# Low parts of expert weights: the last 256 columns of each 1536-column chunk subtracted on GpSimd, the rest on VectorE

## The chip, the core and the metric

The kernel runs on one core of one Trainium2 chip. The metric is the device time of one execution in microseconds (us). In the profile TensorE is PE (its weight loads PEld), VectorE is DVE, ScalarE is ACT, GpSimd is POOL, and SyncE, which issues the large loads, is SP. SBUF is the on-chip memory from which all of them read, PSUM the one into which PE writes.

## The reference

Two layers of a decoder run on 256 positions of width 1024 in float32: attention and a short convolution with a dense feed-forward block, then a gated spatial layer with a feed-forward block of 8 experts, of which each token uses the best two. The part that matters here is the experts:

```python
def expert_block(args):
    xb, e = args
    return (jax.nn.silu(xb @ w1[e]) * (xb @ w3[e])) @ w2[e]
```

For each expert w1 and w3 are 1024x2816 and w2 is 2816x1024. All eight experts together have 277 MB of float32 weights, and every weight is read once.

## The kernel before

To keep float32 accuracy in matmuls of the rounded type `float32r`, each operand is split in two: a high part (the rounded copy) and a low part (the value less its high part). A product is high by high, high by low and low by high.

**The weight stream.** The class `Stream` (L49) brings all weights in, in the order in which PE uses them. SP loads raw tiles of up to 3072 columns (1.5 MB, L126) into a ring, which for the experts has 7 tiles (`RAWA` and `RAWB`). `convert` (L138) takes a raw tile in chunks of 1536 columns (`CVC`): ACT writes the high part `whi` (L153), and DVE subtracts it from the raw weights to give the low part `wlo` (L154). `whi` and `wlo` have four buffers each (`CVA`). `take` (L161) hands 512 or 384 columns at a time to PE. Before it begins a new chunk it calls `convert`, so that conversion is up to four chunks ahead, counting the one that PE is about to use. The chunk that comes four later needs the buffers that PE frees. When the last chunk of a raw tile is converted, `prefetch` (L110) issues the next load into the ring, and that load waits until the tile has been read.

**The experts** (`experts`, L1237) go through 8 experts in three column steps each (1024, 1024 and 768 of the 2816 columns). In each step `up` (L1119) multiplies by w1 and w3, and `down` (L1185) multiplies the step before by w2. Experts 0, 2, 4 and 6 hold up to 128 tokens and take three matmuls for each 512 columns of weights (L447 to L449). Experts 1, 3, 5 and 7 hold up to 64, whose high and low parts lie side by side in one operand, so two matmuls suffice (L1129 and L1130, L1196 and L1197), and the halves are added by `folded` (L1150). A chunk of 1536 columns is thus nine matmuls of 512 columns or six. Besides `wlo`, DVE has small work there on PSUM results: L1145, L1172, L1182, L1210 and L1220. L1168 alone reads two SBUF tiles, as L154 does.

**The order** of DVE, ACT and POOL is fixed by hand from L927 to L1274: each of the three executes in the order of the program text. POOL issues three small loads near the end of the experts (`tail_loads` and `tail_gf`, L1285 to L1290, through L492 and L220) and has nothing else in that stage. After the experts six chunks of 1536 columns for the last projection go through the same stream. Before L913 chunks are converted in two halves of 768 columns (`st.parts` is 2); from there on whole.

Of the kernel before, what the change touches and what calls it, by code (L numbers as in the profile page):

```python
# [10 lines left out]
F32 = mybir.dt.float32  # L11
# [21 lines left out]
CVC = 1536  # L33
RAWA, RAWB = 4, 3
CVA, CVB = 4, 1
# [13 lines left out]
class Stream:  # L49
# [3 lines left out]
    def __init__(self, nc, raws, cvs, cols=RAWC, fixed=None):  # L53
        self.nc, self.raws, self.cvs, self.cols, self.fixed = nc, raws, cvs, cols, fixed
        self.specs, self.loaded, self.n_load = [], [], 0
        self.chunks, self.ready, self.n_conv = [], [], 0
        self.cur, self.pos, self.n_use = None, 0, 0
        self.spare = {}
        self.base, self.ahead, self.parts, self.stop = 0, len(cvs), 1, None

    def add(self, parts, lens):
        i = len(self.specs)
        self.specs.append(parts)
        off = 0
        for n in lens:
            self.chunks.append((i, off, n))
            off += n
# [70 lines left out]
    def convert(self):  # L138
        while self.n_conv < min(self.stop or len(self.chunks), self.n_use + self.ahead):
            ti, off, n = self.chunks[self.n_conv]  # L140
            idx, raw = self.loaded[0]
            assert idx == ti
            base, raw = [u for u in raw if u[0] <= off][-1]
            if self.fixed:
                hi, lo = self.fixed[1]
            else:
                cp = self.cvs[self.n_conv % len(self.cvs)]
                hi = cp.tile([P, CVC], F32R, tag="whi", name="whi")
                lo = cp.tile([P, CVC], F32R, tag="wlo", name="wlo")
            m = self.parts if n % (256 * self.parts) == 0 else 1  # L150
            for i in range(m):
                a, b = n * i // m, n * (i + 1) // m
                self.nc.scalar.activation(hi[:, a:b], raw[:, off - base + a:off - base + b], AF.Copy)  # L153
                self.nc.vector.tensor_sub(lo[:, a:b], raw[:, off - base + a:off - base + b], hi[:, a:b].bitcast(F32))  # L154
            self.ready.append((hi, lo, n))
            self.n_conv += 1
            if self.n_conv == len(self.chunks) or self.chunks[self.n_conv][0] != ti:
                self.loaded.pop(0)
                self.prefetch()
# [14 lines left out]
def decoder_trunk(ctx: ExitStack, tc: tile.TileContext, x, p, positions, ln_mix, ln_ffn, ln_ple, a_w_in,  # L174
# [30 lines left out]
    def bank(name="bank", g="B"):  # L205
        return psp.tile([P, 512], F32, tag="bank" + g, name=name)
# [21 lines left out]
    st = Stream(nc, [(rawp, RAWA)], [cvp] * CVA + [cvp2] * CVB)  # L228
# [572 lines left out]
    for s in range(NSL):  # L801
# [10 lines left out]
        for i in range(len(ab)):  # L812
            n = min(2, nb - 2 * i)
# [24 lines left out]
    for q in range(2):  # L838
        b = bank("wsT")
# [47 lines left out]
    for i in range(4):  # L887
        b = bank("sgp")
# [10 lines left out]
        hi = sg.h[i // 2][:, (i % 2) * 2:(i % 2) * 2 + 2]  # L899
# [15 lines left out]
    st.prefetch()  # L915
    st.stop, st.ahead = None, CVA - 1
    st.convert()
    st.ahead = CVA


    hnh = [t4(dt=F32R, name="hnh") for _ in range(2)]
# [69 lines left out]
    b = bank("rk")  # L991
# [319 lines left out]
    with tc.If(most > 0):  # L1311
# [15 lines left out]
        st = Stream(nc, [], [None], 512, (raws, cvf))  # L1327
# [34 lines left out]
```

## Time and profile before

| what | value |
| --- | --- |
| median of 3 runs | 1207.97 us (1207.48 to 1208.82) |
| profiled execution | 1207.52 us, of which the span of the trace is 1205.3 us |
| busy PE, DVE, ACT, POOL | 1157.8, 974.7, 838.7, 38.5 us |
| data read from HBM | 358.26 MB, 298 GB/s over the span |

The profile is one execution, and its times are from the span's start. A busy PE is not PE at its peak, since ends of matmuls are modelled. A row of a timeline has the start, the duration, the engine, the line and operation, output and inputs with their shapes, how many in a row (x13), and in brackets the engine's idle time before it with what ended it. Instructions of one engine are pipelined: one that is ready begins a little before the end of the one before it, so the spacing of a run of them is shorter than their duration.

### The profile page before, as it was taken

How to read it: one execution, taken by the hardware profiler on the slowest of the kernel's cores; microseconds unless marked ns; L12 is line 12 of the kernel's file. 1: busy time of each engine (PE TensorE's matmuls, PEld its weight loads, DVE VectorE, ACT ScalarE, POOL GpSimd, SP SyncE). 2: the span in 40 equal slices, each digit the busy share in tenths (PEclk: the TensorE clock that was granted, in tenths of full speed). 3: DMA queues.
4: the chain of work that ended last, by engine and by line, in shares of the span. 5: the costliest groups of instructions: out<-in, count | busy, mean ns of one | idle time of the engine just before them, and what ended most of it. 6: DMA issues, size and time to landing. Idle time of an engine off the chain costs nothing.

```text
span 1205.3 us, 16666 instructions
## 1 busy us (share of the span) xinstructions
PE 1157.8 (96%) x6307; PEld 1002.0 (83%) x6307; DVE 974.7 (81%) x1027; ACT 838.7 (70%) x1010; POOL 38.5 (3%) x80
## 2 busy tenths in 40 slices
PE   7999999999999999999999999999999999999985
PEld 5888899998779888888888977888977888987864
DVE  6567756474576778889999989999989999989993
ACT  6645644353466457789887788888788888788864
POOL 1001000000010010000000000000000000000003
PEclk9999999999999979999999999999999999999998
DMA  9634555286546569899999989999989999999921
GB/s 325 222 113 162 195 169 175 89 298 245 163 148 211 209 240 385 334 344 395 403 409 405 407 307 408 399 409 406 397 317 406 377 411 405 398 339 391 395 113 38
DMA packets 112521, 360.46 MB, mean 299 GB/s; under 512 B 6577, under 2 KB 23089, under 8 KB 112434
## 3 DMA queue, kind: packets, MB, share of 16 engines
q1 hardware_dynamic: 110834, 353.56, 77.6%
q0 software_dynamic: 1600, 5.77, 1.5%
q8 instruction: 51, 0.84, 0.3%
q14 instruction: 36, 0.29, 0.1%
HBM read 358.26 MB, written 1.05 MB: 298 GB/s over the span
## 4 chain that ended last, share of the span: by engine, by line
PE 86%; DVE 7%; ACT 2%; issue 2%; POOL 1%; DMA 1%; SPq 0%; POOLq 0%; DVEq 0%; ACTq 0%
DVE wlo L154 4%; PE a L447 3%; PE a L448 3%; PE y L447 3%; PE a L449 3%; PE b L448 3%; PE b L449 3%; PE b L447 3%; PE y L448 3%; PE y L449 3%; PE b L1130 3%; PE gTp L1160 3%; PE y L1197 3%; PE y L1196 3%; PE b L1129 3%; PE a L1130 2%
## 5 line engine op out<-in xcount | busy, mean ns | idle before, releaser
L154 DVE TENSOR_TENSOR wlo<-raw,whi 128x1536 fp32r<-128x1536 f32 (+2 forms) x551 | 770.3, 1444 | 151.3 <-ACT whi L153 148.8
L153 ACT ACTIVATE whi<-raw 128x1536 fp32r<-128x1536 f32 (+2 forms) x551 | 660.8, 1238 | 247.9 <-issue 37.9
L1130 PE MATMUL b<-wlo,xs 128*128 128x512 f32 (+1 forms) x192 | 67.0, 397 | 7.4 <-DVE wlo L154 7.3
L448 PE MATMUL a<-wlo,xg 128*128 128x512 f32 (+1 forms) x192 | 72.0, 375 | 0.0
L449 PE MATMUL a<-whi,xg 128*128 128x512 f32 (+1 forms) x192 | 71.7, 374 | 0.0
L448 PE MATMUL b<-wlo,xg 128*128 128x512 f32 (+1 forms) x192 | 71.2, 371 | 0.0
L449 PE MATMUL b<-whi,xg 128*128 128x512 f32 (+1 forms) x192 | 71.2, 371 | 0.0
L1130 PE MATMUL a<-wlo,xs 128*128 128x512 f32 (+1 forms) x192 | 67.1, 381 | 3.9 <-DVE wlo L154 3.9
L449 PE MATMUL y<-whi,gTe 128*128 128x512 f32 x176 | 68.8, 391 | 0.0
L448 PE MATMUL y<-wlo,gTe 128*128 128x512 f32 x176 | 68.8, 391 | 0.0
L447 PE MATMUL b<-whi,xg 128*128 128x512 f32 (+1 forms) x192 | 68.3, 371 | 0.0
L447 PE MATMUL a<-whi,xg 128*128 128x512 f32 (+1 forms) x192 | 67.7, 378 | 0.0
L447 PE MATMUL y<-whi,gTe 128*128 128x512 f32 x176 | 67.1, 395 | 0.0
L1129 PE MATMUL a<-whi,xs 128*128 128x512 f32 (+1 forms) x192 | 65.9, 374 | 0.0
L1129 PE MATMUL b<-whi,xs 128*128 128x512 f32 (+1 forms) x192 | 63.3, 378 | 0.0
L1197 PE MATMUL y<-wlo,gTe 128*128 128x512 f32 x164 | 58.8, 402 | 0.0
L1196 PE MATMUL y<-whi,gTe 128*128 128x512 f32 x164 | 57.0, 394 | 0.0
L476 PE MATMUL b3p<-hTh,whi 128*128 128x256 f32 x176 | 49.8, 283 | 0.0
L477 PE MATMUL b3p<-hTl,whi 128*128 128x256 f32 x176 | 49.8, 283 | 0.0
L478 PE MATMUL b3p<-hTh,wlo 128*128 128x256 f32 x176 | 49.8, 283 | 0.0
L478 PE MATMUL ap<-hTh,wlo 128*128 128x256 f32 x176 | 49.8, 283 | 0.0
L477 PE MATMUL ap<-hTl,whi 128*128 128x256 f32 x176 | 49.8, 283 | 0.0
(357 smaller groups left out, 2357.1 us busy)
## 6 DMA issues: line engine op xcount, KB each, us to landing
raw<-in_moe_w_dram SPq DMA_DIRECT2D x143, 1536.0 KB, 9.8
raw<-in_moe_w_dram SPq DMA_DIRECT2D x32, 1024.0 KB, 9.0
raw<-in_ffn_w_dram SPq DMA_DIRECT2D x19, 1536.0 KB, 6.7
raw<-in_moe_w_dram SPq DMA_DIRECT2D x32, 512.0 KB, 8.0
raw<-in_a_w_in_dram SPq DMA_DIRECT2D x4, 1536.0 KB, 9.4
raw<-in_ple_gate_dram SPq DMA_DIRECT2D x4, 1536.0 KB, 10.3
raw<-in_c_w_in_dram SPq DMA_DIRECT2D x4, 1536.0 KB, 7.1
raw<-in_a_w_in_dram SPq DMA_DIRECT2D x4, 1024.0 KB, 9.2
```

Source lines behind the costliest of these rows:

```text
L153: self.nc.scalar.activation(hi[:, a:b], raw[:, off - base + a:off - base + b], AF.Copy)
L154: self.nc.vector.tensor_sub(lo[:, a:b], raw[:, off - base + a:off - base + b], hi[:, a:b].bitcast(F32))
L447: T.matmul(o, ah, bh, start=first, stop=False, **kw)
L448: T.matmul(o, ah, bl, start=False, stop=False, **kw)
L449: T.matmul(o, al, bh, start=False, stop=last, **kw)
L476: T.matmul(o, a, tr.hi(k), start=first and c % 512 == 0, stop=False, **kw)
L477: T.matmul(o, a, tr.lo(k), start=False, stop=False, **kw)
L478: T.matmul(o, b, tr.hi(k), start=False, stop=last, **kw)
L1129: T.matmul(ob[:, :w], c["x"][0][k], wh, start=k == 0, stop=False)
L1130: T.matmul(ob[:, :w], c["x"][0][k], wl, start=False, stop=k == 7)
L1196: T.matmul(c["y"][hf], th, wh, start=start, stop=False)
L1197: T.matmul(c["y"][hf], th, wl, start=False, stop=end)
```

## The change

The stream has a new number, `pool`, which is 0 until the first three chunks of the experts are converted and 256 from then on. A chunk of exactly 1536 columns that is converted whole is then divided: DVE subtracts columns 0 to 1279, POOL columns 1280 to 1535. Other chunks (1024 columns) are left to DVE. PE, and the load that reuses the raw tile, now wait for both.

```diff
@@ class Stream, __init__
         self.base, self.ahead, self.parts, self.stop = 0, len(cvs), 1, None
+        self.pool = 0
@@ class Stream, convert
                 self.nc.scalar.activation(hi[:, a:b], raw[:, off - base + a:off - base + b], AF.Copy)
-                self.nc.vector.tensor_sub(lo[:, a:b], raw[:, off - base + a:off - base + b], hi[:, a:b].bitcast(F32))
+                c = b - self.pool if m == 1 and n == CVC else b
+                for eng, a0, b0 in ((self.nc.vector, a, c), (self.nc.gpsimd, c, b)):
+                    if b0 > a0:
+                        eng.tensor_sub(lo[:, a0:b0], raw[:, off - base + a0:off - base + b0],
+                                       hi[:, a0:b0].bitcast(F32))
@@ decoder_trunk, before the experts
     st.stop, st.ahead = None, CVA - 1
     st.convert()
-    st.ahead = CVA
+    st.ahead, st.pool = CVA, 256
```

## Rows read from the trace of the kernel before

**Rows 1.** windows: us, busy time of each engine, granted PE clock, DMA share, GB/s
```profile
437.80:1167.10 729.30, 714.47 (x3528) 606.17 (x3527) 675.00 (x523) 589.30 (x565) 1.92 (x3) 0.99 0.96 372
713.20:808.00 94.80, 90.92 (x452) 75.84 (x451) 92.69 (x64) 82.84 (x75) 0.00 (x0) 1.00 1.02 399
808.00:891.80 83.80, 83.80 (x421) 72.62 (x420) 74.47 (x60) 63.57 (x68) 0.00 (x0) 1.00 0.97 377
780.00:800.00 20.00, 20.00 (x98) 17.11 (x98) 20.00 (x15) 17.39 (x15) 0.00 (x0) 1.00 1.03 410
```

**Rows 2.** DVE by line and shape, 713.2:808.0, then 808.0:891.8
```profile
L154 DVE TENSOR_TENSOR wlo<-raw,whi 128x1536 fp32r<-128x1536 f32 x51 | 86.0, 1751 | 2.4 <-ACT whi L153 2.4
L1168 DVE TENSOR_TENSOR gTe<-gt,gTe 128x512 fp32r<-128x512 f32 x2 | 1.4, 682 | 0.0
L154 DVE TENSOR_TENSOR wlo<-raw,whi 128x1536 fp32r<-128x1536 f32 x37 | 63.7, 1754 | 9.0 <-ACT whi L153 8.9
```

**Rows 3.** timeline of DVE (start us, us, what)
```profile
808.13 1.76 DVE L154 TENSOR_TENSOR wlo<-raw,whi 128x1536 fp32r<-128x1536 f32 x1 [0.28 <-ACT whi L153]
810.17 1.76 DVE L154 TENSOR_TENSOR wlo<-raw,whi 128x1536 fp32r<-128x1536 f32 x1 [0.28 <-ACT whi L153]
891.89 21.78 DVE L154 TENSOR_TENSOR wlo<-raw,whi 128x1536 fp32r<-128x1536 f32 x13 [0.54 <-ACT whi L153]
```

**Rows 4.** waits in 742.7:921.3 (us in total, times, longest), then SP's own
```profile
DVE wlo L154 <- ACT whi L153: 11.3, 17, 4.1
SPq L126 <- DVE wlo L154: 146.1, 44, 7.6
```

**Rows 5.** DVE by line and shape, whole run
```profile
L154 DVE TENSOR_TENSOR wlo<-raw,whi 128x1536 fp32r<-128x1536 f32 x352 | 599.6, 1752 | 56.2 <-ACT whi L153 55.6
L154 DVE TENSOR_TENSOR wlo<-raw,whi 128x512 fp32r<-128x512 f32 x48 | 31.1, 687 | 25.2 <-ACT whi L153 25.1
```

**Rows 6.** POOL by line and shape, whole run
```profile
L357 POOL TENSOR_TENSOR var<-var,ms 128x1 f32<-128x1 f32 x15 | 3.3, 219 | 7.5 <-ACT hgT L932 2.1 <-ACT end L777 1.7 <-ACT sq L400 1.3
```

**Rows 7.** timeline of POOL, then of DVE, from 1186 us on
```profile
1187.01 1.73 POOL L779 TENSOR_TENSOR end<-pps,gain 128x512 f32<-128x512 f32 x1 [3.68 <-DVE pps L775]
1189.36 1.29 POOL L779 TENSOR_TENSOR end<-pps,gain 128x512 f32<-128x512 f32 x1 [0.62 <-DVE pps L775]
1186.89 0.69 DVE L770 TENSOR_TENSOR end<-end,pps 128x512 f32<-128x512 f32 x1
1187.62 1.66 DVE L775 TENSOR_TENSOR pps<-h,end 128x512 f32<-128x512 f32 x1
```

**Rows 8.** timeline of POOL, then of DVE, from 354 us on
```profile
355.07 2.25 POOL L359 TENSOR_TENSOR rstd<-var,mhalf 128x1 f32<-128x1 f32 x1 [0.26 <-POOL var L357]
354.75 0.68 DVE L772 TENSOR_TENSOR h<-h,gate 128x512 f32<-128x512 f32 x1
355.35 0.95 DVE L154 TENSOR_TENSOR wlo<-raw,whi 128x768 fp32r<-128x768 f32 x1
356.22 0.68 DVE L406 TENSOR_TENSOR hg<-h,gain 128x512 f32<-128x512 f32 x1
356.82 0.68 DVE L433 TENSOR_TENSOR hTl<-tp,hTh 128x512 fp32r<-128x512 f32 x1
```

**Rows 9.** timeline of POOL, then of DVE, from 13 us on
```profile
13.76 0.57 POOL L359 TENSOR_TENSOR rstd<-var,mhalf 128x1 f32<-128x1 f32 x1
15.47 0.61 POOL L359 TENSOR_TENSOR rstd<-var,mhalf 128x1 f32<-128x1 f32 x1
15.56 2.11 DVE L433 TENSOR_TENSOR hTl<-tp,hTh 128x512 fp32r<-128x512 f32 x3
```

**Rows 10.** ACT by line and shape, 713.2:808.0
```profile
L153 ACT ACTIVATE whi<-raw 128x1536 fp32r<-128x1536 f32 x52 | 74.9, 1486 | 10.6 <-PE b L1129 2.6 <-PE y L449 2.4 <-PE y L1196 2.0
```

**Rows 11.** timeline of POOL, from 1117 us on
```profile
1117.31 0.82 POOL L492 DMA_DIRECT2D pin<-in_p_dram  x1 [680.50 <-DVE wlo L154]
```

**Rows 12.** window at the start of the experts, columns as in rows 1
```profile
437.80:520.00 82.20, 82.20 (x388) 71.19 (x388) 70.56 (x74) 58.59 (x52) 0.00 (x0) 0.95 0.82 312
```

## The prediction

> **What bounds the kernel now.** I read the windows first. The experts, with the last projection's first loads, fill 437.8 to 1167.1 us: 729 of the span's 1205. DVE is busy 675 us of that, PE 714, DMA has a share of 0.96, and POOL works for 1.9 us [rows 1]. Three resources are near their end at once, so the stage has to be cut finer. It repeats every 178.6 us, once for each pair of experts, and one pair falls into two stretches. In the **saturated stretch** (713.2 to 808.0) DVE is busy for 92.7 of 94.8 us, 51 subtractions of 1536 columns take most of it, and DVE waits for ACT only 2.4 us [rows 1, 2]. A chunk takes 94.8 / 51 = 1.86 us. In the **PE-paced stretch** (808.0 to 891.8) PE is busy throughout, DVE has 9.0 us of waiting before its 37 subtractions, and single ones start 2.04 us apart (810.17 less 808.13), which is PE's nine matmuls [rows 1 to 3]. Six matmuls are then 6/9 of that, 1.36 us. The waits agree: DVE waits little for ACT (11.3 us in one pair), while SP's loads wait for DVE to free raw tiles, 146 us in one pair [rows 4]. So the loads are not late at first, but DMA is close behind: its share is already 1.02 in the saturated stretch, and 410 GB/s with 1.03 is the best 20 us [rows 1]. The run has 352 subtractions of 1536 columns [rows 5], 88 to a pair: four pairs.
>
> **What DVE gives up.** The 13 in a row that end 21.78 us after their start are spaced (21.78 - 1.75) / 12 = 1.67 us [rows 2, 3]. The 512- and 1536-column rows differ by 1.752 - 0.687 = 1.065 us for 1024 columns [rows 5], so 256 columns are 0.27 us and the 1280 that remain are spaced 1.40 us. Two of the 352 chunks stay whole (the first three chunks hold one of 1024 columns and two of 1536), 350 are split: 93 us of DVE work go.
>
> **What POOL takes on.** No row shows a 256-column subtraction there. From below, a two-input POOL operation on one column is 0.22 us [rows 6]; from above, one on 512 columns is 1.29 us when nothing disturbs it, as at 1189.36 [rows 7]. Halfway in columns I take 0.22 + (1.29 - 0.22) / 2 = 0.75 us. That POOL is otherwise idle would make it free, if it ran beside DVE.
>
> **It does not run beside DVE.** The same rows show it. The POOL multiply at 1187.01 takes 1.73 us, not 1.29: DVE's L770, which reads two SBUF tiles, is running until 1187.58. DVE's next, L775, also with two SBUF inputs, then takes 1.66 us where L770 took 0.69, and ends at 1189.28, about one such operation after POOL's end at 1188.74 [rows 7]. They ran one after the other. At 355.07 a POOL operation that takes 0.57 us elsewhere takes 2.25: it ends at 357.32, having let three DVE operations with two SBUF inputs pass (L772, L154, L406), and runs once L433, which reads PSUM, has begun at 356.82 [rows 8, 9]. In a run of such DVE operations POOL is passed over. Beside three L433 at 15.56, with one input in PSUM, POOL's 0.61 us is nearly undisturbed [rows 9]. L154 and its POOL part both read raw and whi, all in SBUF. I therefore count a chunk as 1.40 + 0.75 = 2.15 us of one shared resource, where DVE alone took 1.67.
>
> The Trainium skill states the same as a rule that speaks against this change: in "SBUF — State Buffer", section "Who interferes with whom", a VectorE instruction with two SBUF inputs and a GpSimd one that reads SBUF exclude each other for a whole instruction, and one with at most one SBUF input does not contend; the trace agrees (1.66 us for 0.69). By that rule DVE's work on PSUM could all lie beside POOL's, and the sum would be my lower bound plus the buffer loss below.
>
> **The sum, saturated stretch.** 51 x 2.15 = 109.7 us, and L1168 with two SBUF inputs adds 1.4 [rows 2]: 111.1, which is 16.3 more than 94.8. This is the lower bound if all else hides. A loss comes on top, since the buffers are four deep. When PE waits for POOL's part of chunk k, DVE can have gone to k+3 and no further. POOL then does four parts in 3.0 us; PE finishes k after 0.75 + 1.36 = 2.1 us, and ACT needs 1.49 us for whi of k+4 [rows 10], ready at 3.6. From 3.0 to 3.6 nobody subtracts, 0.6 us for four chunks or five, some 0.13 a chunk: 51 x 0.13 = 6.6. I take 16.3 + 6.6 = 22.9. The upper bound adds DVE's other work of the stretch, 92.7 - 86.0 - 1.4 = 5.3 us [rows 1, 2], which the PSUM rows suggest is mostly beside POOL: 28.2.
>
> **PE-paced stretch.** 37 x 2.15 = 79.6 us fit into 83.8, so from below nothing is lost. From above DVE's other 74.5 - 63.7 = 10.8 us and the loss of 37 x 0.13 = 4.8 come on top: 95.2, that is 11.4 more. PE holds the pace here, so I take a value near the lower end, 2.
>
> **Other edits.** The extra wait of PE and of SP's loads for POOL is in the sum: a late part delays the matmuls, the release of the raw tile and with it the load, but the ring of seven tiles is full (SP waits for DVE), so loads have room and PE is what is late next. POOL's queue now has the three small loads between its parts, 0.82 us for the one shown [rows 11]; each could hold one part back by that, 2.5 us together, covered by the chunks that are ahead, else paid: I take 0. ACT's work is the same. Over four pairs: 4 x (22.9 + 2) = 100 us, bounds 4 x 16.3 = 65 and 4 x (28.2 + 11.4) = 158. The profiled execution took 1207.5, 0.4 under the median, and 2.2 of it lie outside the span. Forecast: **1307 us**, its own range 1272 to 1366.
>
> "GPSIMD Engine Reference" in the Trainium skill, section "Performance versus the Vector engine", gives 4497 ns for a 2048-column add on GpSimd, by which 256 columns would be an estimated 0.56 us; no run here shows that. By it the sum would be some 40 us less.
>
> **Rivals.** *POOL's part lies beside DVE's, or holds it up for less than 0.42 us* (51 x (1.40 + 0.42) + 1.4 = 94.3, the point where the saturated stretch is as now). Then DVE is relieved. PE has 94.8 - 90.9 = 3.9 us of idle time per saturated stretch, 16 in all, and the mean 399 GB/s there against the best 410 allows 2.7%, 10 in all [rows 1]; the PE-paced stretch gains nothing. That gives 1191 to 1198, say 1194. For it: only 0.22 us of fixed cost is seen on POOL, and these rows are multiplies outside the experts. Against it: both directions of blocking in rows 7. 10%.
>
> *The PE clock falls as well.* In 437.8 to 520 the granted clock has a mean of 0.95, against 1.00 in the stretches above [rows 1, 12]; some of that time is spent at the lower of its levels, 1.2 of 2.4 GHz. If PE's new gaps bring it there throughout the saturated stretches, six matmuls take 2 x 1.36 = 2.72 us and replace 2.15 + 0.13 as the pace: 51 x 0.44 x 4 = 90 more, 1397. Against it: gaps of a few us as at present leave 1.00. 8%.
>
> *A cheaper part or more cover*, with blocking: POOL's part at 0.5 us makes the saturated stretch 51 x (1.40 + 0.50 + 0.13) + 1.4 = 104.9, that is 10 more, 40 in all: 1248. 10%. *No change*, where gains and blocking cancel near 0.42 us: 4%.
>
> **How the numbers follow.** The forecast has 68%, the rivals 10, 8, 10 and 4. The range takes in the forecast's bounds and the cheaper part and goes a little towards the clock: 1235 to 1380. 0.2%, some 2.4 us, is about what a measurement of this kernel can tell from no change. Faster by more: 0.10, the first rival. Within: 0.04. Slower: 0.86.
>
> **What would show it.** DVE's `wlo` rows at 128x1280 with a mean well above 1.49 us (that is 1.752 - 0.27), some of them by 0.7; POOL's at 128x256 with a mean above 0.75 and some of several us, where DVE passed it; PE waiting for POOL at L1130; a saturated stretch of some 118 us. Wrong, if DVE's rows stay at 1.49 us and POOL's at one duration, or if PE waits nowhere for POOL. If the time is right but PE's clock shows 0.5 in those stretches, it is right for another reason.

## The result and the profile after

The changed kernel takes 1249.09 us (median of 4 runs, 1248.34 to 1249.97) against 1208.39. The ratio measured is 1.0342, interval 1.0329 to 1.0354; the quotient of the two medians, 1.0337, lies in it. It is 41 us slower, where 100 were forecast. The profiled span grew by 42.5 us, to 1247.8, and POOL is busy for 626 us instead of 38.5.

First the two stretches of one pair of experts, in the windows of the changed kernel (columns as in [rows 1]). The code has moved by a few lines: L154 is L158 now for both engines, L1130 is L1135, L1168 is L1173.

```profile
725.90:829.50 103.60, 95.80 (x458) 75.71 (x457) 102.35 (x64) 84.31 (x76) 90.91 (x52) 1.00 0.99 377
829.50:913.40 83.90, 83.56 (x416) 71.56 (x415) 75.46 (x61) 63.02 (x67) 56.46 (x37) 1.00 0.94 360
```

The saturated stretch went from 94.8 to 103.6 us, with DVE still busy throughout (102.4). The PE-paced one is what it was, 83.9 for 83.8. The bursts of 13 subtractions that open the saturated stretch of two pairs, in the timeline of DVE:

```profile
726.02 24.82 DVE L158 TENSOR_TENSOR wlo<-raw,whi 128x1280 fp32r<-128x1280 f32 x13 [0.82 <-ACT whi L154]
...
913.44 24.84 DVE L158 TENSOR_TENSOR wlo<-raw,whi 128x1280 fp32r<-128x1280 f32 x13 [0.82 <-ACT whi L154]
```

The second burst answers to the one at 891.89 in [rows 3]; the first to this one of the kernel before:

```profile
713.29 21.78 DVE L154 TENSOR_TENSOR wlo<-raw,whi 128x1536 fp32r<-128x1536 f32 x13 [0.54 <-ACT whi L153]
```

A pair of experts takes 913.44 - 726.02 = 187.42 us instead of 178.60, 8.8 more, and the saturated stretch has all of it. Four pairs make 35 of the 42.5 us; the other 7 come at the end.

DVE and POOL in the saturated stretch by line and shape, which answers to [rows 2]:

```profile
L158 DVE TENSOR_TENSOR wlo<-raw,whi 128x1280 fp32r<-128x1280 f32 x51 | 94.5, 1918 | 1.9 <-ACT whi L154 1.9
...
L1173 DVE TENSOR_TENSOR gTe<-gt,gTe 128x512 fp32r<-128x512 f32 x2 | 2.3, 1138 | 0.0
```

```profile
L158 POOL TENSOR_TENSOR wlo<-raw,whi 128x256 fp32r<-128x256 f32 x52 | 91.8, 1793 | 13.8 <-ACT whi L154 11.1 <-PE y L1202 2.7
```

The 51 subtractions have fewer columns (1280 for 1536) and take longer: 1.92 us each for 1.75. L1173, DVE's other operation with two SBUF inputs, went from 0.68 to 1.14. How that comes about is seen in single instructions, two of DVE and then two of POOL:

```profile
788.33 2.02 DVE L158 TENSOR_TENSOR wlo<-raw,whi 128x1280 fp32r<-128x1280 f32 x1
790.28 2.03 DVE L158 TENSOR_TENSOR wlo<-raw,whi 128x1280 fp32r<-128x1280 f32 x1
788.97 1.99 POOL L158 TENSOR_TENSOR wlo<-raw,whi 128x256 fp32r<-128x256 f32 x1
790.92 1.99 POOL L158 TENSOR_TENSOR wlo<-raw,whi 128x256 fp32r<-128x256 f32 x1
```

DVE's subtraction at 788.33 ends at 790.35, POOL's at 788.97 ends at 790.96, and DVE's next, issued at 790.28, ends at 792.31. They take turns: POOL's part sits on its engine for 1.99 us, most of it waiting until DVE's instruction has run, and then DVE's waits until POOL's columns are done. DVE instructions start 1.95 us apart, where they started 1.67 apart before. Over the whole stage DVE's and POOL's subtractions look like this (min/median/max in ns; of the rest of these rows nothing is used):

```profile
L158 DVE TENSOR_TENSOR wlo<-raw,whi x328: 1474/2020/2039, 439.0 to 1148.7; 128x1280 fp32r<-128x1280 f32 x164
...
L158 POOL TENSOR_TENSOR wlo<-raw,whi x328: 732/1981/2107, 447.3 to 1149.1; 128x256 fp32r<-128x256 f32 x164
```

DVE's durations fall into two groups, undisturbed near 1.49 us (92 of the 350) and held up at 2.02 (230), so POOL's part costs DVE 0.53 us when it is in the way. POOL's part lasts 0.73 us when nothing disturbs it. PE's waits, one line each for DVE and POOL as the last to come:

```profile
PE b L1135 <- DVE wlo L158: 15.2, 29, 1.9
...
PEld b L1135 <- POOL wlo L158: 0.6, 2, 0.3
```

PE waits longer than before (15.2 us in the first line, which was 7.3), but by the profile nearly always for DVE: POOL's part is rarely what comes last; it makes DVE late. SP's loads now wait for POOL's reading as well. Over the whole run they name it for 30.7 us, at most 0.6 us at a time, and DVE for 584.8:

```profile
SPq L127 <- POOL wlo L158: 30.7, 59, 0.6
```

### The profile page after: what moved, and what is told of

Same layout as the page of the kernel before. It is cut to its first block, busy times and chain, and to the rows that moved or that the text cites. A ratio compares the mean times of both kernels' runs of the same rounds, so it can differ in the third digit from the quotient of the medians.

```text
span 1247.8 us, 17502 instructions
## 1 busy us (share of the span) xinstructions
PE 1176.7 (94%) x6307; PEld 999.9 (80%) x6307; DVE 1015.9 (81%) x1027; ACT 842.9 (68%) x1010; POOL 626.3 (50%) x430
## 4 chain that ended last, share of the span: by engine, by line
PE 69%; DVE 19%; issue 7%; ACT 3%; DMA 1%; POOL 1%; SPq 0%; DVEq 0%; POOLq 0%; ACTq 0%
DVE wlo L158 16%; PE y L453 3%; PE y L452 3%; PE y L454 3%; PE gTp L1165 3%; PE a L453 2%; PE a L454 2%; PE b L454 2%; PE b L453 2%; PE b L452 2%; PE a L452 2%; PE b L1135 2%; PE xgp L1093 2%; ACT whi L154 2%; PE ap L482 2%
## 5 line engine op out<-in xcount | busy, mean ns | idle before, releaser
L158 DVE TENSOR_TENSOR wlo<-raw,whi 128x1280 fp32r<-128x1280 f32 (+2 forms) x551 | 804.6, 1510 | 149.0 <-ACT whi L154 147.1
L154 ACT ACTIVATE whi<-raw 128x1536 fp32r<-128x1536 f32 (+2 forms) x551 | 663.4, 1239 | 276.0 <-issue 49.4
L158 POOL TENSOR_TENSOR wlo<-raw,whi 128x256 fp32r<-128x256 f32 x350 | 587.9, 1701 | 195.3 <-ACT whi L154 174.8
L360 POOL TENSOR_SCALAR var<-ms 128x1 f32<-128x1 f32 (+1 forms) x16 | 5.2, 328 | 215.8 <-ACT sq L405 93.2
L1135 PE MATMUL b<-wlo,xs 128*128 128x512 f32 (+1 forms) x192 | 68.6, 401 | 15.9 <-DVE wlo L158 15.2
L1135 PE MATMUL a<-wlo,xs 128*128 128x512 f32 (+1 forms) x192 | 67.7, 384 | 8.8 <-DVE wlo L158 8.8
L1135 PEld LDWEIGHTS b<-wlo,xs 128*128 128x128 f32 x192 | 33.3, 189 | 34.3 <-DVE wlo L158 30.4
L1135 PEld LDWEIGHTS a<-wlo,xs 128*128 128x128 f32 x192 | 34.8, 188 | 19.5 <-DVE wlo L158 15.2
```

What stands on the lines that cost most here:

```text
L158: eng.tensor_sub(lo[:, a0:b0], raw[:, off - base + a0:off - base + b0], hi[:, a0:b0].bitcast(F32))
L1135: T.matmul(ob[:, :w], c["x"][0][k], wl, start=False, stop=k == 7)
```

## The experiments

The times below are medians. The kernel before was run again beside these kernels: 1208.25 us beside the first four on record (128 and 512 columns, POOL without reading, the loads one step earlier), 1207.89 beside the other three. Each ratio is the one measured; the quotient of the medians differs from it by 0.0014 at most.

Two theories about the size stood against each other. **A**: a POOL part holds DVE up for its columns alone, and only DVE instructions with two SBUF inputs are held; the loss arises in the saturated stretches. **B**: the hold belongs to the instruction, or the loss comes from waiting for one more engine.

**The number of columns.** Two kernels differ from the changed one in one number.

```diff
-    st.ahead, st.pool = CVA, 256
+    st.ahead, st.pool = CVA, 128
```

> POOL takes 128 columns, DVE 1408. Theory A (a POOL part holds DVE up for its columns alone, 0.545 us for 256, 2.13 ns each, and POOL's fixed part of some 0.19 us goes by unseen): DVE's rows of 1408 columns come as 1.62 us alone or 1.62 + 0.27 = 1.89 us held up; per chunk +0.14 us against the kernel before instead of +0.28, so about half of the loss: 1226 to 1233 us. Theory B (the hold belongs to the instruction and hardly shrinks with its columns): 1.62 + 0.54 = 2.16 us, and a time at or above 1249 us.

```diff
-    st.ahead, st.pool = CVA, 256
+    st.ahead, st.pool = CVA, 512
```

> POOL takes 512 columns, DVE 1024. Theory A: DVE's rows of 1024 columns come as 1.22 us alone or 1.22 + 1.09 = 2.31 us, spaced 2.23 us in the saturated stretches, 51 x 0.28 = 14 us more than at 256 columns in each of four, and a little in the PE-paced ones (37 x 2.23 = 82.5 of 83.8 us): 1305 to 1340 us. Theory B: 1.22 + 0.54 = 1.76 us, spaced 1.68, about as before the change: 1205 to 1220 us.

With 128 columns: 1222.22 us, ratio 1.0123 (1.0106 to 1.0141). With 512: 1315.72 us, ratio 1.0903 (1.0885 to 1.0921). DVE's and POOL's subtractions in the stage, first with 128, then with 512 columns (min/median/max):

```profile
L158 DVE TENSOR_TENSOR wlo<-raw,whi x340: 1211/1875/1912, 447.2 to 1149.9; 128x1408 fp32r<-128x1408 f32 x169, 128x1024 fp32r<-128x1024 f32 x1
...
L158 POOL TENSOR_TENSOR wlo<-raw,whi x338: 458/1837/1952, 446.8 to 1149.7; 128x128 fp32r<-128x128 f32 x169
```

```profile
L158 DVE TENSOR_TENSOR wlo<-raw,whi x301: 1205/2307/2356, 447.2 to 1149.4; 128x1024 fp32r<-128x1024 f32 x151
...
L158 POOL TENSOR_TENSOR wlo<-raw,whi x300: 1286/2269/2396, 446.0 to 1148.4; 128x512 fp32r<-128x512 f32 x150
```

The median of DVE's rows is the held-up one. With 128 columns that is 1.875 us where 1.62 is undisturbed (1.49 plus 128 columns of 1.04 ns, the slope of [rows 5]): a hold of 0.26. With 512 it is 2.31 where 1024 columns alone take 1.22: 1.09. With 0.53 at 256 this is a line through zero, 2.1 ns a column. POOL's undisturbed durations, the minima of its rows, are 0.46, 0.73 and 1.29 us, each about 0.2 longer than its hold. That fixed 0.2 us does not hold DVE up. Theory B's 2.16 and 1.76 us are out. The time with 128 columns is 4 us below the range expected: the loss shrank to a third (14 us for 41), not to a half. In the pair of experts shown above, the 51 chunks of the saturated stretch take 98.1 us from start to start with 128 columns, 103.7 with 256 and 118.1 with 512, where they took 94.8 before: 3.3, 8.8 and 23.3 us more. An estimate of DVE's work in the stretch, with its other work of 1.4 and 5.3 us, tells why this is not in proportion: 51 x 1.67 + 6.7 = 92 us before the change, so that some 3 us were to spare, then 51 x (1.54 + 0.26) + 6.7 = 98.5, 51 x 1.93 + 6.7 = 105 and, with 1.14 + 1.09 = 2.23 a chunk, 120. The loss at the end, told below, is there with 128 columns too: DVE is idle for 3.7 us before L508.

**POOL without reading.** POOL fills its columns with zeros; the low part of 256 of 1536 columns is left out.

```diff
+                self.nc.vector.tensor_sub(lo[:, a:c], raw[:, off - base + a:off - base + c], hi[:, a:c].bitcast(F32))
+                if b > c:
+                    self.nc.gpsimd.memset(lo[:, c:b].bitcast(F32), 0.0)
```

> POOL fills its 256 columns of the low part with zeros instead of subtracting: it writes the same place, waits for the same buffers and PE waits for it, but it reads nothing from SBUF. Left out: the low part of 256 of 1536 columns. Theory A (the two engines' reads exclude each other): no DVE row of 1280 columns is held up, all at 1.48 us; the saturated stretches fall below the 94.8 us of before, 1190 to 1204 us in all. Rival (the loss comes from PE and the loads waiting for one more engine): the time stays above 1230 us.

1193.63 us, ratio 0.9888 (0.9872 to 0.9905): faster than the kernel before. DVE in the stage (min/median/max), then POOL's fills:

```profile
L156 DVE TENSOR_TENSOR wlo<-raw,whi x351: 1215/1489/1495, 446.6 to 1149.3; 128x1280 fp32r<-128x1280 f32 x173, 128x1024 fp32r<-128x1024 f32 x3
```

```profile
L158 POOL MEMSET wlo<- 128x256 f32 x350 | 109.5, 313 | 613.0 <-PE y L452 125.0 <-PE a L452 111.8 <-PE b L452 105.0
```

No subtraction is held up: the longest takes 1.495 us. PE still has to wait for POOL. But a fill reads neither `raw` nor `whi`: it starts when PE has freed the buffer, as its idle time shows, and neither the loads nor ACT wait for it. So this run by itself does not take late loads out of the argument. What does is the changed kernel's own trace: in the saturated stretch DVE is idle for only 103.6 - 102.35 = 1.3 us, and SP's waits hardly name POOL. The fills themselves take 0.31 us. The run also shows what this division could have brought, 14 to 15 us, had POOL's reads been free; the prediction put that at 1194 us in its first rival.

**POOL with one input.** POOL copies its columns of `whi` instead of subtracting; the low part of 256 of 1536 columns is left out again.

```diff
+                self.nc.vector.tensor_sub(lo[:, a:c], raw[:, off - base + a:off - base + c], hi[:, a:c].bitcast(F32))
+                if b > c:
+                    self.nc.gpsimd.tensor_copy(lo[:, c:b], hi[:, c:b].bitcast(F32))
```

> POOL copies its 256 columns of the high part into the low part instead of subtracting: one SBUF input instead of two, the same waits. The low part of 256 of 1536 columns is left out. Theory A as a matter of reads (DVE is held up for as long as POOL reads): DVE rows of 1280 columns at 1.48 us or about half the hold, 1.48 + 0.27 = 1.75 us, and 1205 to 1220 us. Rival (the hold is that of an instruction that reads, whatever it reads): 2.02 us and some 1245 us.

1206.58 us, ratio 0.999 (0.998 to 1.000), as before the change. DVE in the stage:

```profile
L156 DVE TENSOR_TENSOR wlo<-raw,whi x346: 1211/1676/1687, 446.2 to 1146.6; 128x1280 fp32r<-128x1280 f32 x172, 128x1024 fp32r<-128x1024 f32 x1
```

The held-up group lies at 1.676 us, 0.19 over 1.49: the hold follows what POOL reads, and for one input of 256 columns it is shorter than half of the 0.53 for two. It is again about 0.2 us less than POOL's instruction, whose shortest takes 0.40, so the number of inputs and the instruction's duration are not told apart here. DVE is spared 0.27 us a chunk and loses 0.19, so the saturated stretches do gain: 93.4 us for 94.8 in the pair shown above. Near 1140 us the run is 6.2 us ahead of the kernel before, and at its end only 1.9. The late load of `p`, told below, takes most of it back: DVE is idle for 3.43 us before the line that is L508 in the changed kernel.

**Where the loss arises.** POOL takes part only in chunks that are converted in the PE-paced stretches.

```diff
-                c = b - self.pool if m == 1 and n == CVC else b
+                paced = (self.n_conv - 141) % 88 >= 51
+                c = b - self.pool if m == 1 and n == CVC and paced else b
```

> POOL takes 256 columns only in chunks that are converted in the PE-paced stretches (37 of every 88), DVE keeps the whole of the other chunks. Theory A with its loss in the saturated stretches alone: DVE rows held up to 2.02 us are still there, but the time is that of before, 1207 to 1212 us. Rival (each split chunk costs something anywhere): 37/88 of the loss, about 1225 us.

1209.79 us, ratio 1.0017 (1.0007 to 1.0026). DVE over the whole run:

```profile
L159 DVE TENSOR_TENSOR wlo<-raw,whi 128x1536 fp32r<-128x1536 f32 x205 | 346.4, 1750 | 19.4 <-ACT whi L154 19.1
L159 DVE TENSOR_TENSOR wlo<-raw,whi 128x1280 fp32r<-128x1280 f32 x147 | 254.1, 1767 | 38.0 <-ACT whi L154 38.0
```

147 chunks are split and their mean is 1.77 us, not 1.49, so many are held up, and yet the time grows by 2 us. Had every split chunk cost the same, it would be 37/88 of 41, that is 17. The run also lacks the loss at the end, about 7 us, since POOL has no subtraction ahead of its load of `p` (issued at 1119.93, told below). The rest of the loss sits in the saturated stretches, as theory A has it.

**The end of the experts.** POOL's three small loads at the end are issued in program order, now behind its subtractions. In the changed kernel, POOL first, then DVE:

```profile
1187.33 2.04 POOL L158 TENSOR_TENSOR wlo<-raw,whi 128x256 fp32r<-128x256 f32 x1 [3.83 <-ACT whi L154]
1189.32 0.82 POOL L497 DMA_DIRECT2D pin<-in_p_dram  x1
...
1187.29 3.43 DVE L158 TENSOR_TENSOR wlo<-raw,whi 128x1280 fp32r<-128x1280 f32 x2 [0.82 <-ACT whi L154]
1194.50 0.69 DVE L508 TENSOR_TENSOR pT<-pT 128x512 fp32r<-128x512 f32 x1 [3.78 <-ACT pT L507]
```

The same operation of DVE in the kernel before, then a piece of the chain that sets the changed kernel's time:

```profile
1154.89 0.68 DVE L503 TENSOR_TENSOR pT<-pT 128x512 fp32r<-128x512 f32 x1
```

```profile
1189.32 3.30 DMA pin<-in_p_dram
```

The load of `p` (`pin`, at 1117.31 in [rows 11]) is issued at 1189.32. Of these 72 us some 35 are the delay of everything by then, the rest is POOL's queue. DVE sits idle for 3.8 us before L508, which needs what PE and ACT make of `pin`; before the change it had no idle time there. The experiment puts the first two loads one step earlier in the program.

```diff
-    experts(steps, rank, st, ctxs, {(NE - 1, 2): [tail_loads, tail_p, tail_gf]})
+    experts(steps, rank, st, ctxs, {(NE - 1, 1): [tail_loads], (NE - 1, 2): [tail_p, tail_gf]})
```

> As changed, but the three columns of jobs at the end are parted: the two loads that POOL issues first (p and the gain of the last projection) stand one step earlier in the program. If the late load of p is what cost the end of the experts 3.8 us of DVE idle (it is issued at 1189.3 us instead of 1117.3 us): 1244 to 1246 us. Rival (the chain at the end is held by the subtractions anyway): 1249 us, as changed.

1241.88 us, ratio 1.0278 (1.0259 to 1.0297): 7 us less than the changed kernel, about twice what was expected. POOL's load, then DVE:

```profile
1158.70 0.82 POOL L497 DMA_DIRECT2D pin<-in_p_dram  x1
...
1187.59 1.49 DVE L158 TENSOR_TENSOR wlo<-raw,whi 128x1280 fp32r<-128x1280 f32 x1 [0.82 <-ACT whi L154]
1189.00 0.68 DVE L508 TENSOR_TENSOR pT<-pT 128x512 fp32r<-128x512 f32 x1
```

The load goes out at 1158.70, and L508 follows the subtraction ahead of it without a gap. The move also changed the order of PE's matmuls at the end somewhat, so that the gain beyond 3.8 us is not put down to the load alone. With this, 34 us of loss are left, and four times 8.8 is 35. The two traces agree: near 1144 us of the kernel before, both are 35 us behind it; at the end the changed kernel is 42.5 behind and this one 36.1.

**A version faster than both.** If only DVE instructions with two SBUF inputs are in POOL's way, POOL should work while DVE reads PSUM. In each saturated stretch POOL takes 896 columns of the one chunk ahead of L1220's four additions and 512 of the one ahead of L1210's pair, eight chunks in the run. POOL first copies one column that DVE writes in the same chunk, which makes it start after DVE's part and not in the middle of earlier subtractions.

```diff
-                self.nc.vector.tensor_sub(lo[:, a:b], raw[:, off - base + a:off - base + b], hi[:, a:b].bitcast(F32))
+                c = b - self.pool.get(self.n_conv, 0)
+                for eng, a0, b0 in ((self.nc.vector, a, c), (self.nc.gpsimd, c, b)):
+                    if b0 > a0:
+                        if a0 > a:
+                            eng.tensor_copy(self.mark, lo[:, 0:1].bitcast(F32))
+                        eng.tensor_sub(lo[:, a0:b0], raw[:, off - base + a0:off - base + b0],
+                                       hi[:, a0:b0].bitcast(F32))
...
+    st.ahead, st.mark = CVA, cst.tile([P, 1], F32, name="mark")
+    st.pool = {**{154 + 88 * i: 512 for i in range(4)}, **{160 + 88 * i: 896 for i in range(4)}}
```

> POOL takes part only where DVE's next work reads PSUM: 896 columns of the one chunk ahead of the four additions into h, 512 columns of the one ahead of the two outputs y, in the saturated stretches (eight chunks in all, the same ones in each pair of experts); a copy of one column makes POOL begin after DVE's part. Theory A (only DVE instructions with two SBUF inputs exclude POOL): the parts run beside that work, DVE is relieved of 0.93 + 0.53 us in each stretch, 4 x 1.5 = 6 us: 1202 to 1206 us, faster than both kernels. Rival (PE then waits for the long POOL part, or the part slips behind a DVE subtraction): 1208 to 1214 us.

1201.51 us (5 runs), ratio 0.9947 (0.9934 to 0.9961): 6.4 us, or half a percent, faster than the kernel before. One saturated stretch, with a chunk of 1024 columns for DVE at 737.37, DVE and then POOL (L1218 is L1210 of before, L1228 is L1220):

```profile
737.37 1.23 DVE L160 TENSOR_TENSOR wlo<-raw,whi 128x1024 fp32r<-128x1024 f32 x1 [1.09 <-ACT whi L154]
738.52 1.40 DVE L1218 SCALAR_TENSOR_TENSOR y<-y,gg 128x512 fp32r<-128x512 f32 x2
739.84 0.88 DVE L1176 TENSOR_TENSOR gTe<-gt,gTe 128x512 fp32r<-128x512 f32 x1
...
749.72 2.47 DVE L1228 TENSOR_TENSOR h<-cb,h 128x512 f32<-128x512 f32 x4
...
738.87 1.30 POOL L160 TENSOR_TENSOR wlo<-raw,whi 128x512 fp32r<-128x512 f32 x1
...
750.07 2.13 POOL L160 TENSOR_TENSOR wlo<-raw,whi 128x896 fp32r<-128x896 f32 x1
```

POOL's parts last 1.30 and 2.13 us, which is their undisturbed length (512 columns took 1.29), and beside them L1218 twice in 1.40 us and L1228 four times in 2.47 us are as long as in the stretch of the kernel before:

```profile
L1220 DVE TENSOR_TENSOR h<-cb,h 128x512 f32<-128x512 f32 x4 | 2.5, 680 | 0.0
L1210 DVE SCALAR_TENSOR_TENSOR y<-y,gg 128x512 fp32r<-128x512 f32 x2 | 1.4, 742 | 0.0
```

Neither holds the other up. Only where POOL's part outlasts this work is there a hold again: the first part ends at 740.17, and L1176 (L1168 of before, two SBUF inputs), which begins at 739.84, takes 0.88 us for 0.68. The stretch, in the windows:

```profile
712.50:806.00 93.50, 90.88 (x452) 75.89 (x451) 91.04 (x66) 82.80 (x75) 3.70 (x4) 1.00 1.01 399
```

It takes 93.5 us where it took 94.8 [rows 1].

## Why the prediction was right and where it was wrong

**Right: the mechanism and the sign.** DVE and POOL exclude each other when both read two SBUF tiles, as [rows 7] said; the two-group durations and the run without reading show it. The loss lies in the saturated stretch; the PE-paced stretch absorbs it (2 us forecast per pair, 0.1 measured). The falling PE clock did not come: the granted clock is 1.00 in both stretches, although PE has more gaps. The signs named for DVE's and POOL's rows came in kind, DVE's smaller (0.53 where 0.7 was expected); of POOL's 350 rows just one is longer than 2.2 us, where several us were expected of some; PE was to be seen waiting for POOL, and the profile names DVE; the saturated stretch takes 103.6 us, where some 118 were expected.

**Wrong: the price of POOL's part.** "I therefore count a chunk as 1.40 + 0.75 = 2.15 us of one shared resource, where DVE alone took 1.67." The 0.75 was the duration of POOL's instruction, right as such (0.73 measured), but only 0.53 of it holds DVE up. The other 0.2 us may go by while POOL waits for its turn; no run shows where. Taken with the spacing, a chunk costs 1.95 us, and 51 of them 10 us less than reckoned. Some parts also ran beside DVE's work on PSUM, so that the mean was lower still: the 51 subtractions took 94.5 us for the 109.7 in the sum, 15 less. L1173 is a small term on the other side: it was counted at 1.4 us for two instructions, is held up as well (1.14 us each), and there is a third, of 384 columns, that the sum left out (1.09 us).

**Wrong: the loss at the buffers.** It rested on "In a run of such DVE operations POOL is passed over". In the stream POOL was not: it gets its turn after each subtraction. So PE does not have to run dry before POOL can start, and DVE is idle for only 103.6 - 102.35 = 1.3 us of the stretch. 6.6 us were reckoned.

**Wrong: the edit costed at nothing.** POOL's own loads were bounded by how long each would hold back a subtraction, 2.5 us. The cost came the other way round: the subtractions hold back a load. It is in the last 7 us, and the end of the experts is on the chain that sets the time. Had the price been 0.53 and the buffer loss 0, the sum would have been 51 x 1.93 + 1.4 - 94.8 = 5 us for each stretch with all other work hidden, and 10 with DVE's 5.3 us on top; 8.8 lies between. Of the 24.9 us that were forecast for a pair 8.8 came, 64 us less over four pairs, and the end put 7 back: 43 for 100.

**Luck.** The measured 1249 us lies next to the rival "A cheaper part or more cover", 1248 at 10%, but that agreement is in part chance. The rival's price of 0.50 us is close to the measured 0.53. It kept the 0.13 us of buffer loss, which did not come, and had neither DVE's other work in the stretch nor the loss at the end, which did.

"GPSIMD Engine Reference" in the Trainium skill, section "Performance versus the Vector engine", gives 4497 ns for 2048 columns; by that an estimate in proportion is 0.56 us for 256. That is nearer to the measured hold, 0.53, than to the measured duration, 0.73.

## What to carry to other kernels

A second engine relieves the first only where their instructions do not hold each other up: here, where both read two SBUF tiles, each column moved from DVE to POOL spared 1.04 ns and cost 2.1 ns, so more of it was worse (14, 41 and 108 us in all at 128, 256 and 512 columns), while the same work placed beside instructions that read PSUM gained 6 us. Price such a move by the hold that the busy engine feels, not by the duration of the other's instruction, and only in the stretch where the busy engine is the bound. And look at what else the receiving engine's queue holds in program order: a small load behind the new work cost about 7 us at the end here, a sixth of the loss.

## What the runs showed of the hardware that had not been expected

A GpSimd subtraction of two SBUF tiles held VectorE up by 2.1 ns a column and no fixed amount (0.26, 0.53 and 1.09 us at 128, 256 and 512 columns), a GpSimd copy by 0.19 us for 256 columns, a GpSimd fill not at all. "SBUF — State Buffer" in the Trainium skill, section "Who interferes with whom", lets an instruction that only writes go free; the fill agrees. The same page of the Trainium skill, section "SBUF: two separate sides", states the lock for the whole instruction; here 0.53 of 0.73 us was measured, and the measurement decides. Where the prediction cites the page for instructions with at most one SBUF input, it leaves out the page's condition that they run outside the 2-port perf modes; no run here bears on that condition.

Who goes next is not settled. Between two subtractions of the stream POOL got its turn; at 355 us POOL was passed over three times [rows 8]. It happened again in the changed kernel, after the experts, DVE first, then POOL:

```profile
1206.09 2.49 DVE L411 TENSOR_TENSOR hg<-h,gain 128x512 f32<-128x512 f32 x4
1208.49 1.49 DVE L158 TENSOR_TENSOR wlo<-raw,whi 128x1280 fp32r<-128x1280 f32 x1
1209.90 2.65 DVE L438 TENSOR_TENSOR end<-tp,end 128x512 fp32r<-128x512 f32 x4
...
1206.96 4.30 POOL L158 TENSOR_TENSOR wlo<-raw,whi 128x256 fp32r<-128x256 f32 x2 [8.98 <-ACT whi L154]
```

The first of these two POOL parts takes 3.61 us and ends at 1210.57: L411 and the subtraction, all with two SBUF inputs, pass it undisturbed, and it is done 0.67 us after L438, which reads PSUM, begins. Ahead of the stream's subtractions DVE executes a wait for a semaphore, and at 355 us the trace has none between the three. That alone is not the difference: the subtraction at 1208.49 has such a wait too, executed at 1206.22. The cause stays open.
